# The last pair of forgetting-attention heads turned through VectorE and DRAM instead of on TensorE, with the filling jobs dealt anew

## The chip, the cores and the metric

The kernel runs on one core of one Trainium2 chip. The metric is device time in microseconds (us) for one launch; the median of three runs is compared. Engines are named as in the profile: PE is TensorE (PEld its weight loads), DVE is VectorE, ACT is ScalarE, POOL is GpSimd, SP is SyncE, which here only issues DMAs.

## The reference

One layer of a streaming encoder over 512 tokens of width 1024. Four token mixers run on the same normed input: differential attention (branch a), forgetting attention (branch f), a Conformer convolution (c) and a short gated convolution (d). Each is projected to 1024 channels, gated and summed; a cross-attention and a gated MLP follow. The part that the change touches is branch f, eight heads of width 64:

```python
c = jnp.cumsum(log_f, axis=1)                       # log_f: log-sigmoid of a gate column, per head
s = jnp.einsum('bqhd,bkhd->bhqk', q_blk, k) * scale
s = s + c_blk[..., None] - c_k[:, :, None, :]
p = jax.nn.softmax(jnp.where(mask, s, -jnp.inf), axis=-1)   # mask: key <= query
return jnp.einsum('bhqk,bkhd->bqhd', p, v)
...
proj = jnp.einsum('bsnc,ncd->bsnd', br, w_branch)   # br: the four branches, 512 channels each
gates = jax.nn.sigmoid(h @ w_gate + b_gate)
mixed = jnp.sum(gates * proj, axis=2) @ w_out
```

All is float32. The kernel gets this precision by splitting each factor into a high and a low part and multiplying three times (high by high, high by low, low by high).

## The kernel before

**Jobs.** `run_blocks` goes through a list of jobs. A typical job loads one 512 KB piece of weights (SP, tile `wr`, two buffers), splits it (ACT writes `wh` at L198, DVE writes `wl` at L199, four buffers each), and runs 24 matmuls of 128x128 by 128x512 (L241) into PSUM. Weights are fetched three jobs ahead.

**Background tasks.** Attention heads are generators, `f_task(p)` for a pair p of heads and `a_task(h)`, that are stepped between jobs by `Background`: it keeps a clock that advances with each matmul traced, pays a task's step from a credit, and takes up a step only when the delay that the last step gave has passed. At most two tasks are stepped at a time. `bg.drain` issues all the remaining steps of a task in one go. This settles the program order; a list scheduler then places each engine's instructions in a static order, by program order among what its own timeline holds ready. On the chip each engine, and SP's queue of DMAs, works strictly in that order.

**Forgetting attention.** `mixer_jobs` yields, for each pair p, two jobs that make the queries and keys (`kv_blocks(p)`; the second adds `f_task(p)`), and between the pairs jobs of branch a's gates and projection (`gate_blocks(0, "a")`, twelve jobs: twice a gate job and then a projection job, four times over). Before, three of them stand after pair 1, three after pair 2, six after pair 3, and then the drain of branch f. A step of `f_task` below 4 makes the scores of one strip of 128 queries against its (step+1)*128 keys for both heads: POOL makes the bias (L1123, L1125), PE the scores (`ps_sc`), DVE adds and finds the row extremum (L1129), ACT exponentiates (L1135), DVE and ACT normalise (L1137 to L1142). The strip, queries by keys, lies in a tile `e`, of which there are three buffers in all.

**Two ways of turning a strip.** The value product needs keys on the partitions. Pairs 0 to 2 (`far`) go a long way round: DVE transposes 32x32 squares (`turn_squares`, L854) into another `e`, `put` (L859) writes it to DRAM from SP, `get` (L866) reads it back in an order that finishes the turn, into `ptl`, and `split_in_place` makes the high part `pth` (ACT, L872) and the low part in place (DVE, L873). Pair 3 goes the short way: `to_keys_major` transposes each 128x128 block on PE into a bank `tr` (L247) and splits it out of PSUM (ACT L161, DVE L162). `GETS` and `SPLITS` say at which of the eight steps the strips are read back and split; the short way has six steps. `pth` and `ptl` have two buffers, one for each head of the pair, and hold two strips: strips 0 and 1, then 2 and 3.

**The end of a pair.** `values` multiplies the turned strips into two banks `av`, first strips 0 and 1, then 2 and 3. A last step adds each bank's halves (ACT copy L1153, DVE add L1154) and splits the pair's 128 channels into `y["f"]` (L161, L162).

**PSUM banks.** A job's bank comes from a rotation, `turn_of.among`. In this stretch it is `("mm", "mm", "tr0")`: two banks `mm` and one that the PE turns would use. Pair 3 sets it to `("mm")` at its step 2, as it needs both `tr` banks. After the drain come the jobs of the last branch, `last_branch_jobs`: two gate jobs of branch f, then `share("mm", "av")`, and then a projection job over `y["f"]` (two banks, each accumulated over four blocks of channels, one for each pair of heads), two gate jobs, and so on. A gate job's result goes to a tile `ge`, of two buffers, that its projection frees.

Of the kernel before, what the change touches and what calls it, by code (L numbers as in the profile page):

```python
# [83 lines left out]
def hybrid_layer(ctx: ExitStack, tc: tile.TileContext, a: dict, out: bass.AP):  # L84
# [21 lines left out]
    def share_now(*among):  # L106
        vars(turn_of).update(n=1, among=among)
# [102 lines left out]
    steps_of = []  # L210
# [654 lines left out]
    def get(d, n, pt, local):  # L865
        SP.dma_start(part_of(pt[1], n, local).bitcast(F32), d.rearrange("(a j) (b x) -> (j b) a x", j=32, b=4))  # L866

    def split_in_place(n, pt, local):
        hi, lo = (part_of(x, n, local) for x in pt)
        raw = lo.bitcast(F32)  # L870
        with tc.issue_after(evacuations[0]):
            A.copy(hi, raw)  # L872
        V.tensor_tensor(lo, raw, hi.bitcast(F32), ALU.subtract)  # L873
# [21 lines left out]
    def pt_tiles():  # L895
        return tuple(m1p.tile([P, 2, 4, 4, 32], F32R, tag=n, name=n, bufs=2) for n in ("pth", "ptl"))

    GETS, SPLITS = {3: (0, 1), 5: (2, 3)}, {4: (0, 1), 6: (2, 3)}
# [158 lines left out]
    f_steps = {-1: 8}  # L1057

    def f_task(p, qk, v):
        f_steps[p] = 0  # L1060
        far = p < 3
        while f_steps[p - 1] < 4:
            yield 0.0, 0.5
        ck = []
        for j in range(2):
            t = m1p.tile([P, S], F32, tag="ck", name="ck", bufs=2)
            G.dma_start(t, crows[2 * p + j:2 * p + j + 1, :].rearrange("a s -> (a s)").partition_broadcast(P))
            ck.append(t)
        yield 0.0, 2.0 if p else 5.0
        es, pts, av, ready = {}, None, None, []  # L1070

        def turn_ready():
            while ready:
                qt, e, w = ready.pop()
                turned = e4()
                for j in range(2):
                    turn_squares(turned[:, j, :w], e[:, j, :w])
                es[qt] = put(turned, w)
        for step in range(8 if far else 6):
            if step in ((5, 7) if far else (3, 5)):  # L1080
                if av is None:
                    av = [bank("av"), bank("av")]
                with tc.issue_after(steps_of[0]) if far else ExitStack():
                    for j in range(2):
                        hl = v[0][:, :, 2 * p + j]
                        values(av[j], lambda kt: ((hl[:, kt], 0), (hl[:, kt], 1)), pts[j],
                               step // 2 - (2 if far else 1))
            while step == (3 if far else 2) and f_steps[p - 1] < 8:
                yield 0.0, 0.5
            f_steps[p] = step + 1  # L1090
            cost = 0.0
            if step == 4:
                turn_ready()
            if far:
                for qt in SPLITS.get(step, ()):
                    for j in range(2):
                        split_in_place(qt + 1, pts[j], qt % 2)
                    cost += 0.1 + 0.3 * qt
                for qt in GETS.get(step, ()):
                    if qt % 2 == 0:  # L1100
                        pts = [pt_tiles() for _ in range(2)]
                    d = es.pop(qt)
                    for j in range(2):
                        get(d[:, j], qt + 1, pts[j], qt % 2)
            else:
                if step == 2:
                    share_now("mm")
                for qt in {2: (0, 1), 3: (2,), 4: (3,)}.get(step, ()):
                    if qt % 2 == 0:
                        pts = [pt_tiles() for _ in range(2)]  # L1110
                    e = es.pop(qt)
                    for j in range(2):
                        to_keys_major(e[:, j], qt + 1, pts[j], qt % 2)
                    cost += 0.4 + 0.3 * qt
            if step < 4:
                qt, w = step, (step + 1) * P
                e = es[qt] = e4()
                st = m1p.tile([P, 8], F32, tag="st8", name="st8", bufs=4)
                for j in range(2):
                    head = 2 * p + j  # L1120
                    bias = m1p.tile([P, S], F32, tag="fbias", name="fbias", bufs=2)

                    G.tensor_scalar(bias[:, :w], ck[j][:, :w], -1.0, cq[:, qt, head:head + 1],  # L1123
                                    ALU.mult, ALU.add)
                    G.affine_select(out=bias[:, w - P:w], in_=bias[:, w - P:w], pattern=[[-1, P]],  # L1125
                                    compare_op=ALU.is_ge, fill=BIG, base=0, channel_multiplier=1)
                    ps = bank("sc")
                    scores(ps, qk, j, qt * P, w)
                    low = V.tensor_tensor_reduce(e[:, j, :w], ps[:, :w], bias[:, :w], scale=-HD ** -0.5,  # L1129
                                                 scalar=3.0e38, op0=ALU.add, op1=ALU.min,  # L1130
                                                 accum_out=st[:, j:j + 1])
                with tc.issue_after(low.ins):
                    turn_ready()
                for j in range(2):
                    A.activation(e[:, j, :w], e[:, j, :w], AF.Exp, bias=st[:, j:j + 1],  # L1135
                                 scale=-1.0, accum_out=st[:, 4 + j:5 + j])
                V.reciprocal(st[:, 6:8], st[:, 4:6])  # L1137
                for j in range(2):
                    if j:
                        V.tensor_scalar(e[:, j, :w], e[:, j, :w], st[:, 6 + j:7 + j], None, ALU.mult)  # L1140
                    else:
                        A.activation(e[:, j, :w], e[:, j, :w], AF.Copy, scale=st[:, 6 + j:7 + j])  # L1142
                cost += 0.6 + 0.0038 * w
                if far:
                    ready.append((qt, e, w))
                    cost += 0.003 * w
            yield cost, 6.5 if far and step == 5 else 4.5
        if "f" not in y:
            y["f"] = (y8(), y8())

        e = e4()
        for j in range(2):
            A.copy(e[0:HD, j], av[j][HD:P])  # L1153
            V.tensor_tensor(e[j * HD:(j + 1) * HD, 0], av[j][0:HD], e[0:HD, j], ALU.add)  # L1154
        split(e[:, 0], y["f"][0][:, p], y["f"][1][:, p])
        yield 1.8, 0.0
# [45 lines left out]
    def mixer_jobs():  # L1202
        yield from c_jobs()
        yield then(lambda: bg.add(lam_task(), "lam"))
        yield from d_jobs()
        yield then(lambda: bg.add(conv_norm_task(), "conv"))
        wide = m1p.tile([P, NT, D], F32, tag="v", name="wide")
        free = iter([wide[:, i] for i in (0, 1, 2, 3) * 2])
        ns.out_sums = out_sums = Sums(w_out, NK // 2, lambda: next(free), SP, "out_sums")
        steps = {5: (out_sums.load, 0), 6: (out_sums.load, 1), 9: (out_sums.add, 0), 10: (out_sums.store, 0),  # L1210
                 11: (out_sums.add, 1)}
        for i, job in enumerate(gate_blocks(3, "d")):
            yield job
            if i in steps:
                yield then(lambda f=steps[i]: f[0](f[1]))
        yield then(lambda: y.pop("d"))
        vj = v_jobs(O_AV, va)
        yield then(lambda: (out_sums.store(1), out_sums.load(2), out_sums.load(3)) and None)
        for f, q in ((out_sums.add, 2), (out_sums.add, 3)):
            yield next(vj)  # L1220
            yield then(lambda f=f, q=q: f(q))
            yield then(lambda q=q: out_sums.store(q))
        yield from vj
        yield share("mm", "mm", "tr0")
        gc = gate_blocks(2, "c")
        for h, n in enumerate((0, 2, 4, 6)):
            yield from qk_jobs(O_AQ, O_AK, h, lambda qk, h=h: bg.add(a_task(h, qk, va), "a"))
            if n:
                yield then(lambda: bg.drain("conv"))
            for _ in range(n):  # L1230
                yield next(gc)
        yield then(lambda: bg.drain("a"))
        yield from vf_jobs(vf)
        yield from kv_blocks(0)
        ga = gate_blocks(0, "a")
        for p in range(1, 4):
            yield from kv_blocks(p)
            for _ in range((3, 3, 6)[p - 1]):
                yield next(ga)
        yield then(lambda: bg.drain("f"))  # L1240

# [656 lines left out]
```

## Time and profile before

| | |
|---|---|
| median of three runs | 1047.57 us (1047.52 to 1048.46) |
| the profiled execution's own time | 1047.26 us |
| its span, first to last instruction | 1045.5 us |
| PE busy | 1035.8 us, 5235 matmuls |
| DVE busy | 809.6 us |
| ACT busy | 510.6 us |
| POOL busy | 143.3 us |
| granted PE clock | 0.999 |
| pair 3's stretch, from its first scores to its last addition | 479.6 to 520.7 us |

Busy time counts each instruction from its start to its end, overlaps once; for PE, whose matmuls are pipelined, the distance between starts says more of what one costs than its duration. A time without a row's shape is a mean over shapes. "Idle before, releaser" in a row names what an engine waited for.

### The profile page before, as it was taken

How to read it: one execution, taken by the hardware profiler on the slowest of the kernel's cores; microseconds unless marked ns; L12 is line 12 of the kernel's file. 1: busy time of each engine (PE TensorE's matmuls, PEld its weight loads, DVE VectorE, ACT ScalarE, POOL GpSimd, SP SyncE). 2: the span in 40 equal slices, each digit the busy share in tenths (PEclk: the TensorE clock that was granted, in tenths of full speed). 3: DMA queues.
4: the chain of work that ended last, by engine and by line, in shares of the span. 5: the costliest groups of instructions: out<-in, count | busy, mean ns of one | idle time of the engine just before them, and what ended most of it. 6: DMA issues, size and time to landing. Idle time of an engine off the chain costs nothing.

```text
span 1045.5 us, 14417 instructions
## 1 busy us (share of the span) xinstructions
PE 1035.8 (99%) x5235; PEld 880.7 (84%) x5235; DVE 809.6 (77%) x1241; ACT 510.6 (49%) x838; POOL 143.3 (14%) x239
## 2 busy tenths in 40 slices
PE   9999999999999999999999999999999999999997
PEld 8888888888888988888888899998888888888886
DVE  7999998677787367878577898777767777667786
ACT  5322222376565365666444566555343333445662
POOL 4001000100010123342101031121112111111001
PEclk9999999999999999999999999999999999999999
DMA  8954333334433246666338744135676676626662
GB/s 271 311 156 100 101 101 101 91 91 121 142 104 109 62 122 178 184 165 158 120 124 287 237 134 127 62 108 184 193 240 229 214 227 217 220 82 183 216 214 82
DMA packets 187453, 166.48 MB, mean 159 GB/s; under 512 B 20415, under 2 KB 159148, under 8 KB 187381
## 3 DMA queue, kind: packets, MB, share of 16 engines
q1 hardware_dynamic: 178339, 133.80, 43.1%
q10 hardware_dynamic: 6482, 23.21, 6.1%
q0 software_dynamic: 2560, 8.54, 2.7%
q8 instruction: 41, 0.67, 0.3%
q14 instruction: 31, 0.25, 0.1%
HBM read 140.74 MB, written 24.79 MB: 158 GB/s over the span
## 4 chain that ended last, share of the span: by engine, by line
PE 99%; DMA 0%; DVE 0%; issue 0%; POOL 0%; POOLq 0%; DVEq 0%; SPq 0%; ACT 0%; ACTq 0%
PE ps_mm L241 47%; PE ps_av L241 30%; PE ps_tr L241 11%; PE ps_sc L241 7%; PE ps_tr L247 2%; PE ps_mm L459 1%; PE ps_av L459 1%; DMA xs<-in_x 0%; PE ps_tr L443 0%; DVE o L1788 0%; PE ps_av L443 0%; DVE nt L438 0%; DVE ge L1183 0%; DVE nt L412 0%; POOL st_m L285 0%
## 5 line engine op out<-in xcount | busy, mean ns | idle before, releaser
L198 ACT CAST wh<-wr 128x1024 fp32r<-128x1024 f32 (+1 forms) x140 | 146.5, 1047 | 233.5 <-PE ps_mm L241 121.2
L199 DVE TENSOR_TENSOR wl<-wr,wh 128x1024 fp32r<-128x1024 f32 (+1 forms) x140 | 174.8, 1249 | 86.2 <-ACT wh L198 85.4
L241 PE MATMUL ps_mm<-hth,wh 128*128 128x512 f32 (+1 forms) x536 | 198.9, 378 | 0.0
L241 PE MATMUL ps_mm<-htl,wh 128*128 128x512 f32 (+1 forms) x536 | 198.3, 377 | 0.0
L241 PE MATMUL ps_mm<-hth,wl 128*128 128x512 f32 (+1 forms) x536 | 198.3, 377 | 0.0
L241 PE MATMUL ps_av<-hth,wh 128*128 128x512 f32 (+1 forms) x328 | 122.5, 374 | 0.0
L241 PE MATMUL ps_av<-htl,wh 128*128 128x512 f32 (+1 forms) x328 | 122.5, 373 | 0.0
L241 PE MATMUL ps_av<-hth,wl 128*128 128x512 f32 (+1 forms) x328 | 122.3, 373 | 0.0
L241 PEld LDWEIGHTS ps_mm<-hth,wl 128*128 128x128 f32 x536 | 99.0, 188 | 18.3
L241 PEld LDWEIGHTS ps_mm<-hth,wh 128*128 128x128 f32 x536 | 99.0, 188 | 17.9 <-ACT hth L161 0.3
L241 PEld LDWEIGHTS ps_mm<-htl,wh 128*128 128x128 f32 x536 | 98.9, 188 | 17.9
L694 DVE SCALAR_TENSOR_TENSOR y<-y,par,y 128x508 f32<-128x508 f32 (+29 forms) x120 | 82.5, 725 | 0.1
L241 PEld LDWEIGHTS ps_av<-hth,wh 128*128 128x128 f32 x328 | 61.6, 188 | 11.1 <-DVE e L1154 0.3
L241 PEld LDWEIGHTS ps_av<-htl,wh 128*128 128x128 f32 x328 | 61.6, 188 | 10.9
L241 PEld LDWEIGHTS ps_av<-hth,wl 128*128 128x128 f32 x328 | 61.6, 188 | 10.9
L1689 DVE TENSOR_TENSOR wl<-dw,wh 128x1024 fp32r<-128x1024 f32 x32 | 40.2, 1260 | 15.0 <-ACT wh L1688 14.7
L1688 ACT CAST wh<-dw 128x1024 fp32r<-128x1024 f32 x32 | 33.4, 1051 | 22.2 <-PE ps_mm L241 7.4
L1636 ACT ACTIVATE th<-c 128x512 f32<-128x512 f32 x22 | 13.9, 632 | 48.8 <-DVE c L621 48.8
L1123 POOL TENSOR_SCALAR fbias<-ck,cq 128x128 f32<-128x128 f32 (+3 forms) x32 | 23.4, 739 | 73.0 <-DVE st L1129 66.6
L621 DVE SCALAR_TENSOR_TENSOR c<-ps_mm,par,c 128x510 f32<-128x510 f32 (+1 forms) x44 | 32.7, 744 | 0.7
L241 PE MATMUL ps_tr<-hth,wh 128*128 128x512 f32 x80 | 31.8, 398 | 0.0
L241 PE MATMUL ps_tr<-htl,wh 128*128 128x512 f32 x80 | 31.6, 395 | 0.0
(503 smaller groups left out, 2227.9 us busy)
## 6 DMA issues: line engine op xcount, KB each, us to landing
wr<-in_w_up SPq DMA_DIRECT2D x44, 512.0 KB
wr<-in_w_in SPq DMA_DIRECT2D x38, 512.0 KB
wr<-in_w_gate SPq DMA_DIRECT2D x32, 512.0 KB
wp<-in_w_down ACTq DMA_DIRECT2D x22, 512.0 KB
sums<-wp ACTq DMA_DIRECT2D x22, 512.0 KB
dw<-sums SPq DMA_DIRECT2D x44, 256.0 KB
wr<-in_w_branch SPq DMA_DIRECT2D x16, 512.0 KB
wide<-in_w_out SPq DMA_DIRECT2D x12, 512.0 KB
```

Of the source, the lines that this page charges most:

```text
L198: last_weights[:] = [order(A.copy(hi, raw[:, :n])).ins, low.tensor_tensor(lo, raw[:, :n], hi.bitcast(F32), ALU.subtract).ins]
L199: low.tensor_tensor(lo, raw[:, :n], hi.bitcast(F32), ALU.subtract).ins]
L241: steps_of[:] = [PE.matmul(ps, lhs, rhs, start=start, stop=stop).ins]
L247: turns.append(PE.transpose(ps, x, ident[:n, :n]).ins)
L459: keep(PE.matmul(banks[c][:, :S // 2], w[p == 1][:, k, c * P:(c + 1) * P], ht[p == 2][:, i * 4 + k, :S // 2], start=(i, p, k) == (0, 0, 0) ...
L621: ins = V.scalar_tensor_tensor(dst[:, s:], src[:, :S - s], w(k), dst[:, s:], ALU.mult, ALU.add)
L694: ins = V.scalar_tensor_tensor(dst[:, s:], src[:, :S - s], pc("conv_dw", k * 4 + j), dst[:, s:], ALU.mult, ALU.add)
L1123: G.tensor_scalar(bias[:, :w], ck[j][:, :w], -1.0, cq[:, qt, head:head + 1], ALU.mult, ALU.add)
L1636: A.activation(th, c[:, 0], AF.Silu)
L1688: A.copy(hi, x)
L1689: V.tensor_tensor(lo, x, hi.bitcast(F32), ALU.subtract)
```

## The change

Pair 3 takes the long way like the others: the short branch of `f_task` is gone, with its PE turns and its change of the bank rotation, and the task has eight steps with the delays of the others. The gate and projection jobs of branch a are dealt out two, three and seven in place of three, three and six, so that one job moves from behind pair 1 to behind pair 3 and the pairs 2 and 3 are begun one job earlier.

```diff
     def f_task(p, qk, v):
         f_steps[p] = 0
-        far = p < 3
...
-        for step in range(8 if far else 6):
-            if step in ((5, 7) if far else (3, 5)):
+        for step in range(8):
+            if step in (5, 7):
                 if av is None:
                     av = [bank("av"), bank("av")]
-                with tc.issue_after(steps_of[0]) if far else ExitStack():
+                with tc.issue_after(steps_of[0]):
                     for j in range(2):
                         hl = v[0][:, :, 2 * p + j]
                         values(av[j], lambda kt: ((hl[:, kt], 0), (hl[:, kt], 1)), pts[j],
-                               step // 2 - (2 if far else 1))
-            while step == (3 if far else 2) and f_steps[p - 1] < 8:
+                               step // 2 - 2)
+            while step == 3 and f_steps[p - 1] < 8:
                 yield 0.0, 0.5
...
-            if far:
-                for qt in SPLITS.get(step, ()):
...
-            else:
-                if step == 2:
-                    share_now("mm")
-                for qt in {2: (0, 1), 3: (2,), 4: (3,)}.get(step, ()):
-                    if qt % 2 == 0:
-                        pts = [pt_tiles() for _ in range(2)]
-                    e = es.pop(qt)
-                    for j in range(2):
-                        to_keys_major(e[:, j], qt + 1, pts[j], qt % 2)
-                    cost += 0.4 + 0.3 * qt
+            for qt in SPLITS.get(step, ()):
+                for j in range(2):
+                    split_in_place(qt + 1, pts[j], qt % 2)
+                cost += 0.1 + 0.3 * qt
+            for qt in GETS.get(step, ()):
+                if qt % 2 == 0:
+                    pts = [pt_tiles() for _ in range(2)]
+                d = es.pop(qt)
+                for j in range(2):
+                    get(d[:, j], qt + 1, pts[j], qt % 2)
...
-                cost += 0.6 + 0.0038 * w
-                if far:
-                    ready.append((qt, e, w))
-                    cost += 0.003 * w
-            yield cost, 6.5 if far and step == 5 else 4.5
+                ready.append((qt, e, w))
+                cost += 0.6 + 0.0068 * w
+            yield cost, 6.5 if step == 5 else 4.5
...
         for p in range(1, 4):
             yield from kv_blocks(p)
-            for _ in range((3, 3, 6)[p - 1]):
+            for _ in range((2, 3, 7)[p - 1]):
                 yield next(ga)
```

The tables and functions of the long way, which the change leaves as they are:

```python
GETS, SPLITS = {3: (0, 1), 5: (2, 3)}, {4: (0, 1), 6: (2, 3)}

def put(e, w):
    ...
    SP.dma_start(d, e[:, :, :w])
    return d
def get(d, n, pt, local):
    SP.dma_start(part_of(pt[1], n, local).bitcast(F32), d.rearrange("(a j) (b x) -> (j b) a x", j=32, b=4))
```

More of the change, by code (lines that the diff above doesn't have):

```diff
@@ L1093, in f_task @@
                 turn_ready()
-            if far:
-                for qt in SPLITS.get(step, ()):
-                    for j in range(2):
-                        split_in_place(qt + 1, pts[j], qt % 2)
-                    cost += 0.1 + 0.3 * qt
-                for qt in GETS.get(step, ()):
-                    if qt % 2 == 0:
-                        pts = [pt_tiles() for _ in range(2)]
-                    d = es.pop(qt)
-                    for j in range(2):
-                        get(d[:, j], qt + 1, pts[j], qt % 2)
-            else:
-                if step == 2:
-                    share_now("mm")
-                for qt in {2: (0, 1), 3: (2,), 4: (3,)}.get(step, ()):
-                    if qt % 2 == 0:
-                        pts = [pt_tiles() for _ in range(2)]
-                    e = es.pop(qt)
-                    for j in range(2):
-                        to_keys_major(e[:, j], qt + 1, pts[j], qt % 2)
-                    cost += 0.4 + 0.3 * qt
+            for qt in SPLITS.get(step, ()):
[8 more added lines that the diff above has]
+                    get(d[:, j], qt + 1, pts[j], qt % 2)
             if step < 4:
```

## The prediction

> **What bounds the kernel now.** I read the page first, then the stretches around pair 3, then PE's waits.
>
> ```profile
> span 1045.5 us, 14417 instructions
> PE 1035.8 (99%) x5235; PEld 880.7 (84%) x5235; DVE 809.6 (77%) x1241; ACT 510.6 (49%) x838; POOL 143.3 (14%) x239
> PE 99%; DMA 0%; DVE 0%; issue 0%; POOL 0%; POOLq 0%; DVEq 0%; SPq 0%; ACT 0%; ACTq 0%
> ```
>
> PE is busy for 99% of the span and the chain that ended last is 99% PE. Stretch by stretch (columns: sum of the stretch, then PE, PEld, DVE, ACT, POOL, clock, DMA share):
>
> ```profile
> 480.00:490.00 10.00, 10.00 (x48) 8.33 (x48) 8.52 (x19) 4.89 (x12) 4.72 (x8) 1.00 0.90 232
> 490.00:500.00 10.00, 10.00 (x55) 8.63 (x54) 8.09 (x19) 6.91 (x16) 4.53 (x6) 1.00 0.45 122
> 500.00:510.00 10.00, 10.00 (x55) 8.43 (x53) 6.68 (x13) 6.93 (x14) 0.00 (x0) 1.00 0.55 161
> 510.00:520.00 10.00, 10.00 (x57) 8.55 (x56) 3.51 (x5) 3.33 (x5) 0.00 (x0) 1.00 0.18 52
> ```
>
> PE is full in all four. DVE has 1.5 us of 10 to spare at first and 6.5 at the end; the DMA engines fall from 0.90 to 0.18. What PE waited for in the whole run near this place is two weight loads:
>
> ```profile
> PEld ps_mm L241 <- DVE ge L1183: 0.5, 1, 0.5
> PEld ps_av L241 <- DVE e L1154: 0.3, 1, 0.3
> ```
>
> So here an edit counts in two ways only: by the PE time that it takes away, and by any moment at which PE, which follows a fixed order, is made to wait.
>
> **The change part by part.** *The PE turns go.* The chain of waits over 488 to 530 us shows them as pieces of the time that decides:
>
> ```profile
> 491.67 0.22 PE ps_tr L247 x2
> 500.23 0.22 PE ps_tr L247 x2
> 501.16 0.22 PE ps_tr L247 x2
> 506.60 0.35 PE ps_tr L247 x3
> 508.52 0.35 PE ps_tr L247 x3
> 510.50 0.44 PE ps_tr L247 x4
> 514.63 0.44 PE ps_tr L247 x4
> ```
>
> 2 x (1+2+3+4) = 20 transposes in seven pieces, 3 x 0.22 + 2 x 0.35 + 2 x 0.44 = 2.24 us. All of it is on the path. If both waits above went as well (0.5 + 0.3), the saving would be 3.0 us; I count none of them and take 2.3. By the Trainium skill, page "TensorE: Matmul & The Clock Gate", section "Part 4: PE-mode transpose", one 128x128 transpose costs about 275 ns in a kernel; an estimate from that is 20 x 0.275 = 5.5 us. The pieces say 0.11 each, because transposes overlap one another here, so the sum goes by the pieces.
>
> *The squares come.* DVE turns each strip of each head, by these rows:
>
> ```profile
> L854 DVE STREAM_TRANSPOSE e<-e 128x512 f32<-128x512 f32 x3 | 3.2, 1082 | 0.0
> L854 DVE STREAM_TRANSPOSE e<-e 128x384 f32<-128x384 f32 x2 | 1.6, 852 | 0.4 <-DMA turned<-e 0.4
> L854 DVE STREAM_TRANSPOSE e<-e 128x256 f32<-128x256 f32 x2 | 1.2, 621 | 0.0
> L854 DVE STREAM_TRANSPOSE e<-e 128x128 f32<-128x128 f32 x2 | 0.7, 382 | 0.0
> ```
>
> 2 x (1.082 + 0.852 + 0.621 + 0.382) = 5.87 us more on DVE, between about 484 and 506 us. DVE's idle time from 490 to 520 is 1.9 + 3.3 + 6.5 = 11.7 us, so I cost them at nothing on PE as a load; as a delay they are in the tail below. If the cover were gone, the low parts of weights (L199) behind them would come late. The splits are exchanged one for one, out of SBUF in place of PSUM: nothing.
>
> *Four writes and eight reads come on SP's queue.* At the rows' 0.36 to 0.5 us of issue (below) some 5 us in a queue that issues one or two weight loads in 10 us: nothing while weights are ahead.
>
> *The dealing and the banks.* The twelve jobs of branch a are the same matmuls in another order, and PE is full on both sides of the move: nothing. What it does is start pair 3 sooner. I followed the planner's arithmetic (matmuls, costs, delays as written in the code): pair 3's strips 0 and 1 are taken up half a job earlier than before, strip 2 before the drain instead of in it. Strip 3, the first value product of pair 3 and the second one of pair 2 stay in the drain. One gate job in `tr0` instead of `mm` saves at most the 0.5 us wait above and costs nothing that the trace shows.
>
> *The tail decides.* After the drain PE fills its time with the last branch: two gate jobs, half a projection (nine matmuls into an `mm` bank), a third gate job into the other `mm` bank. Then it needs an `av` bank, and pair 3 holds both until its sums are read.
>
> ```profile
> 515.37 0.28 PE L241 MATMUL ps_av<-pth,v 128*128 128x256 f32 x1
> 518.58 0.69 PE L241 MATMUL ps_av<-y,wh 128*128 128x512 f32 x2
> 517.16 0.58 ACT L1153 COPY e<-ps_av 64x512 f32<-64x512 f32 x1 [1.47 <-PE ps_av L241]
> 517.77 0.68 DVE L1154 TENSOR_TENSOR e<-ps_av,e 64x512 f32<-64x512 f32 x1 [1.36 <-ACT e L1153]
> ```
>
> The first `av` bank is free at 517.77 + 0.68 = 518.45, and PE enters it at 518.58: the slack is 0.1 us. With 2.24 us less to do PE is there at 516.3. If the bank is free by then the saving stays; each us later costs one.
>
> When is it free on the long way? The rows I go by:
>
> ```profile
> 501.10 0.69 DVE L1129 CUSTOM_DVE_ANT_0 e<-ps_sc,fbias 128x512 f32<-128x512 f32 x1 [0.17 <-PE ps_mm L241]
> 494.83 2.85 POOL L1123 TENSOR_SCALAR fbias<-ck,cq 128x512 f32<-128x512 f32 x2 [4.87 <-DVE st L1129]
> 393.08 0.37 SPq L859 DMA_DIRECT2D turned<-e  x1
> 396.09 0.92 SPq L866 DMA_DIRECT2D ptl<-turned  x2
> 403.63 0.91 SPq L866 DMA_DIRECT2D ptl<-turned  x2
> 405.77 0.41 ACT L872 CAST pth<-ptl 128x256 fp32r<-128x256 f32 x1 [2.49 <-DMA ptl<-turned]
> 481.98 0.37 SPq L859 DMA_DIRECT2D turned<-e  x1
> 486.27 0.91 SPq L866 DMA_DIRECT2D ptl<-turned  x2
> 490.79 0.62 ACT L872 CAST pth<-ptl 128x512 fp32r<-128x512 f32 x1 [1.71 <-DMA ptl<-turned]
> 506.05 4.10 SPq L182 DMA_DIRECT2D wr<-in_w_gate  x2
> ```
>
> Before, strip 3's scores were added at 501.10 just after the PE turns of strip 1 (501.16 in the chain) gave back one of the three `e` buffers. Squares give it back sooner, so strip 3 is held only by its bias, ready near 494.83 + 2.85 + 0.6 = 498.3; with a share of DVE's queue its scores are done near 499.0. Then, by the three `e` buffers: squares of strip 2 (2 x 0.85) to 500.7; pair 2's closing additions and split (0.58 and 0.68 twice, then 0.62 and 0.69, overlapped: 3.4) to 504.1; squares of strip 3 (2 x 1.08) to 506.3; a write and a read, X; cast 0.62, low part 0.69, eight value matmuls 0.95, then 0.58 and 0.68 and a hand-over of 0.1. That is 506.3 + X + 3.6 = 509.9 + X, and PE waits when X is over 6.4 us.
>
> X has two ends. Light: a write of strip 0 from 393.08 to its read at 396.09, 3.0, and a read from 403.63 to its cast at 405.77, 2.1: X = 5.1, free at 515.0. Loaded: 481.98 to 486.27 and on to 490.79, 8.8: free at 518.7, a wait of 2.4 and a saving of about nothing. The loaded rows were taken at a DMA share of 0.90; pair 3's last strip will travel between 506 and 515, where before has 0.55 falling to 0.18. It is nearer to light, though its 512 KB are four times strip 0's; I take X near 6 and no wait.
>
> The sum: 2.3 us off the profiled execution's 1047.26 (span 1045.5 and 1.76 around it) is 1044.96; the median stands 0.31 above that execution, so 1047.57 - 2.3 = **1045.3 us**.
>
> **The rivals.** *Turned into a wait.* X between 6.4 and 10.7 us, or the same lateness in any link: the wait eats the saving to the point where it is 2.1 us worse, 1045.5 to 1049.7; at X = 8.8, 1047.7. For it: slack in this tail is 0.1 us now, and ACT already waits 1.71 and 2.49 us for such reads, so the fixed order thinks them quicker than they are. Against: DMA and DVE empty out after 500 us.
>
> *Slower: the read of the last strip is stuck in SP's queue.* SP issues in order, and the second of two loads at 506.05 goes out only some 3.7 us after the first, when a `wr` buffer is free. If strip 3's write or read stands behind such a load, X is 8.8 + 4.1 = 12.9, the bank is free at 522.8, PE stands for 6.5 us, less 2.3: 1051.8 us. It decides from X = 10.8 on. For it: three buffers of `e`, two of `wr`, one queue. Against: three heads of branch a and three pairs went this way, and PE's waits name no read and no split of theirs, though none of them had the end of branch f behind it. By the Trainium skill, page "VectorE: DVE Perf Modes", section "Rules for kernel authors", a 128x128 transpose belongs on TensorE where PSUM will do, which is the path given up here; the trace agrees on the engines' time (four blocks 1.08 us on DVE, 0.44 on PE), and says that DVE has that time to spare.
>
> *The transposes cost their full duration.* If PE's pieces understate them by the page's figure named above, the saving would be 5.5 us, 1042.1 us. The seven pieces speak against it.
>
> **How the numbers follow.** No wait (1044.5 to 1045.4): 0.50. Turned into a wait: 0.24. Slower: 0.23, a third of it below 1050.0. Full duration: 0.03. The range 1044.3 to 1050.0 leaves out the last and two thirds of the slower case, 0.03 + 0.15; the likeliest case's own range is 1044.3 to 1045.4. A measurement of this kernel can tell about 0.2%, 2.1 us, from no change. Faster by more: 0.50 + 0.03 = 0.53; within: 0.24; slower by more: 0.23.
>
> **What would show it.** These rows of before change:
>
> ```profile
> L247 PE MATMUL ps_tr<-ident,e x66: 201/272/301, 284.5 to 514.8; 128*128 128x128 f32 x62, 8*128 8x8 f32 x4
> L854 DVE STREAM_TRANSPOSE e<-e x36: 358/738/1115, 238.6 to 480.9; 128x128 f32<-128x128 f32 x9, 128x256 f32<-128x256 f32 x9, 128x384 f32<-128x384 f32 x9, 128x512 f32<-128x512 f32 x9
> L866 SPq DMA_DIRECT2D ptl<-turned x36: 359/440/1007, 240.7 to 486.7; - x36
> L859 SPq DMA_DIRECT2D turned<-e x24: 332/359/456, 239.1 to 482.0; - x24
> ```
>
> In the profile after: twenty fewer L247 of `ps_tr<-ident,e` (66 to 46), eight more L854 of `e<-e` (36 to 44), four more L859 and eight more L866; PE busy near 1033.5. Right: no PE wait over 0.5 us between 490 and 530, and pair 3's first L1153 by 515.2 us. Turned into a wait: PEld waiting for DVE L1154 or ACT L872 there. Slower: a PE gap of 4 us or more, with L866 of strip 3 issued after 511 behind a `wr` load. I am wrong altogether if PE's busy time does not fall, or if the time is lost before 490 us, where only the dealing acts.

## The result, and the profile after

The changed kernel takes 1054.97 us (median of four runs, 1054.06 to 1055.49) against 1047.55 for the kernel before: a ratio of 1.0070, 95% interval 1.0057 to 1.0083. It is 7.4 us slower. 1045.3 was forecast, and the range ended at 1050.0.

From the page of the changed kernel: span, busy times, the chain that ended last.

```profile
span 1053.2 us, 14415 instructions
PE 1037.5 (99%) x5215; PEld 880.9 (84%) x5215; DVE 813.9 (77%) x1249; ACT 510.8 (49%) x838; POOL 140.6 (13%) x239
PE 95%; DMA 2%; DVE 2%; issue 1%; SPq 0%; ACT 0%; POOL 0%; POOLq 0%; DVEq 0%; ACTq 0%
```

The span is 7.7 us longer. PE runs twenty matmuls fewer (5215 for 5235) and is yet busy 1.7 us longer. The chain that was PE for 99% is now 2% DMA and 2% DVE. The work itself changed as the code says; these rows, by line and shape (column after the count: shortest, mean and longest in ns), answer to the last four of the prediction:

```profile
L247 PE MATMUL ps_tr<-ident,e x46: 201/272/294, 284.6 to 382.1; 128*128 128x128 f32 x42, 8*128 8x8 f32 x4
L854 DVE STREAM_TRANSPOSE e<-e x44: 367/731/1120, 238.7 to 508.3; 128x128 f32<-128x128 f32 x11, 128x256 f32<-128x256 f32 x11, 128x384 f32<-128x384 f32 x11, 128x512 f32<-128x512 f32 x11
L866 SPq DMA_DIRECT2D ptl<-turned x44: 359/458/1637, 240.7 to 515.1; - x44
L859 SPq DMA_DIRECT2D turned<-e x28: 332/359/1179, 239.1 to 509.4; - x28
```

Up to 500 us PE is full in both traces. By stretches (sum of the stretch, then PE, PEld, DVE, ACT, POOL, clock, DMA share, GB/s):

```profile
500.00:510.00 10.00, 8.95 (x40) 6.62 (x38) 5.32 (x9) 6.57 (x15) 0.00 (x0) 1.00 0.55 173
510.00:520.00 10.00, 8.16 (x37) 6.30 (x37) 3.76 (x6) 1.86 (x4) 0.00 (x0) 1.00 0.99 249
520.00:530.00 10.00, 7.46 (x23) 5.83 (x24) 4.45 (x6) 3.67 (x6) 0.00 (x0) 0.66 0.17 52
```

From 500 us on PE is no longer full, the DMA share in 510 to 520 is 0.99 where before had 0.18, and in the last stretch the granted clock is 0.66. What PE's weight loads waited for between 490 and 535 us (total, times, longest):

```profile
PEld ps_av L241 <- ACT pth L872: 3.8, 4, 1.8
PEld ps_av L241 <- DVE ptl L873: 2.7, 4, 1.4
PEld ps_av L241 <- DVE e L1140: 1.2, 1, 1.2
PEld ps_mm L241 <- DVE y L162: 0.2, 1, 0.2
```

7.9 us in all, nearly all of it at pair 3's value products and at the projection behind them: high parts, low parts, the closing addition (L1140 is the old L1154; lines behind `f_task` moved up by 12 to 14). In the chain over 520 to 540 us stands the other loss:

```profile
523.31 0.60 DVE e L1140
523.96 8.47 PE ps_av L241 x24
535.84 2.72 PE ps_mm L241 x12
```

The twelve matmuls from 535.84 take 0.227 us each; 24 of them would take 5.44, and the 24 from 523.96 took 8.47: 3.0 us of halved clock. The sum: 2.2 saved, 7.9 - 0.8 = 7.1 of new waits, 3.0 of slow clock, together 7.9 longer by this count, and 7.7 by the spans. The split between waits and clock is rough: by the pages PE idles 6.0 us more (1053.2 - 1037.5 against 1045.5 - 1035.8) and is busy 1.7 us more, although its work shrank by 2.2.

Where the lateness comes from is read from the chain over 505 to 523 us, then from the timeline of that stretch for ACT, DVE, PE and POOL:

```profile
499.79 7.43 DMA turned<-e
...
509.36 3.06 DMA turned<-e
512.44 0.36 SPq L866
512.89 0.57 SPq L182
513.55 1.47 SPq L866
515.08 5.39 DMA ptl<-turned
```

```profile
504.22 0.30 ACT L872 CAST pth<-ptl 128x128 fp32r<-128x128 f32 x1 [3.38 <-DMA ptl<-turned]
504.54 1.07 ACT L1139 COPY e<-ps_av 64x512 f32<-64x512 f32 x2
504.55 0.29 DVE L873 TENSOR_TENSOR ptl<-ptl,pth 128x128 fp32r<-128x128 f32 x1 [3.51 <-ACT pth L872]
507.24 2.09 DVE L854 STREAM_TRANSPOSE e<-e 128x512 f32<-128x512 f32 x2 [0.23 <-DMA turned<-e]
517.10 0.62 ACT L872 CAST pth<-ptl 128x512 fp32r<-128x512 f32 x1 [0.32 <-DMA ptl<-turned]
520.49 0.62 ACT L872 CAST pth<-ptl 128x512 fp32r<-128x512 f32 x1 [0.17 <-DMA ptl<-turned]
521.16 0.39 PE L241 MATMUL ps_av<-pth,v 128*128 128x256 f32 x1 [1.63 <-ACT pth L872]
522.08 0.58 ACT L1139 COPY e<-ps_av 64x512 f32<-64x512 f32 x1
```

```profile
497.82 0.57 POOL L1252 DMA_DIRECT2D g_mem<-in_norm_mem  x1 [2.02 <-PE ps_sc L241]
498.57 0.54 POOL L1286 DMA_DIRECT2D m_t<-in_mem  x1 [0.17 <-issue]
```

Strip 2's write is issued at 499.79 and lands 7.43 us later, beside two 512 KB loads of the cross-attention's memory that POOL issued at 497.82 and 498.57. Its source is one of the three `e` buffers, so strip 3's squares could not start before it landed; they start at 507.24. The write is the last thing that they wait for, but by 0.23 us only. ACT meanwhile stands 3.38 us for a small read, with pair 2's closing copies behind it (504.54), and DVE stands 3.51 us for that cast (504.55), with pair 2's closing additions and the squares behind it.

From the end of the squares the chain runs on: 3.1 us for strip 3's write, 2.7 us (512.42 to 515.08) in which SP issues two other reads and a weight load, 5.4 us for the last read. At the end ACT casts head 0's last strip at 517.10, stands for head 1's reads, casts a weight, and only then copies the first `av` bank, at 522.08. PE's own order holds it up as well: head 1's value products stand ahead of the next projection, and the first of them waits 1.63 us for head 1's cast (521.16).

### The profile page after: what moved, and what is told of

The parts are those of the page before. It is cut to its first block, busy times and chain, and to the rows that moved or that the text cites. A ratio compares the mean times of both kernels' runs of the same rounds, so it can differ in the third digit from the quotient of the medians.

```text
span 1053.2 us, 14415 instructions
## 1 busy us (share of the span) xinstructions
PE 1037.5 (99%) x5215; PEld 880.9 (84%) x5215; DVE 813.9 (77%) x1249; ACT 510.8 (49%) x838; POOL 140.6 (13%) x239
## 4 chain that ended last, share of the span: by engine, by line
PE 95%; DMA 2%; DVE 2%; issue 1%; SPq 0%; ACT 0%; POOL 0%; POOLq 0%; DVEq 0%; ACTq 0%
PE ps_mm L241 44%; PE ps_av L241 30%; PE ps_tr L241 11%; PE ps_sc L241 7%; PE ps_tr L247 2%; DMA turned<-e 1%; PE ps_mm L459 1%; PE ps_av L459 1%; DMA ptl<-turned 1%; DMA xs<-in_x 0%; DVE e L854 0%; DVE wl L199 0%; ACT wh L198 0%; DVE ptl L873 0%; SPq L866 0%
## 5 line engine op out<-in xcount | busy, mean ns | idle before, releaser
L241 PE MATMUL ps_mm<-hth,wh 128*128 128x512 f32 (+1 forms) x528 | 195.3, 377 | 0.0
L241 PE MATMUL ps_mm<-htl,wh 128*128 128x512 f32 (+1 forms) x528 | 195.1, 377 | 0.0
L241 PE MATMUL ps_mm<-hth,wl 128*128 128x512 f32 (+1 forms) x528 | 195.0, 377 | 0.0
L241 PE MATMUL ps_tr<-hth,wh 128*128 128x512 f32 x88 | 34.8, 396 | 0.0
L241 PE MATMUL ps_tr<-htl,wh 128*128 128x512 f32 x88 | 34.7, 395 | 0.0
L241 PE MATMUL ps_tr<-hth,wl 128*128 128x512 f32 x88 | 34.7, 394 | 0.0
L873 DVE TENSOR_TENSOR ptl<-ptl,pth 128x128 fp32r<-128x128 f32 (+3 forms) x44 | 20.5, 499 | 16.9 <-ACT pth L872 16.7
```

The lines of the kernel that those rows point to most:

```text
L241: steps_of[:] = [PE.matmul(ps, lhs, rhs, start=start, stop=stop).ins]
```

## The experiments

Each was compared with the kernel before on its own chip: ratio (95% interval), median in us.

| run | edit | median | ratio |
|---|---|---|---|
| deal_only | before, dealt 2, 3, 7 | 1047.49 | 0.9998 (0.9988 to 1.0007) |
| far_336 | after, dealt 3, 3, 6 | 1056.38 | 1.0077 (1.0062 to 1.0092) |
| mem_late | after, memory loads later in program order | 1056.01 | 1.0071 (1.0054 to 1.0088) |
| pace_30 | after, shorter delays in all steps | 1052.45 | 1.0043 (1.0028 to 1.0058) |
| lead_55 | after, one delay 1 us shorter | 1049.57 | 1.0016 (1.0007 to 1.0026) |
| mem_late2 | after, memory loads on SP behind a later weight load | 1051.20 | 1.0034 (1.0021 to 1.0047) |
| own_tile | after, strip 3's squares in tiles of their own | 1054.46 | 1.0062 (1.0047 to 1.0077) |
| warm | after, ten filler matmuls in the waits | 1053.54 | 1.0052 (1.0036 to 1.0069) |
| comb | lead_55 and mem_late2 | 1045.39 | 0.9978 (0.9969 to 0.9987) |
| two_comb | comb, two gate jobs before the drain | 1046.67 | 0.9994 (0.9985 to 1.0003) |
| last_pe | after, strip 3 turned on PE | 1046.91 | 0.9995 (0.9986 to 1.0003) |
| last_pe_lead | last_pe and lead_55 | 1053.39 | 1.0054 (1.0041 to 1.0067) |
| before_comb | before, with comb's two edits | 1052.72 | 1.0039 (1.0027 to 1.0051) |
| comb_336 | comb, dealt 3, 3, 6 | 1052.24 | 1.0043 (1.0030 to 1.0056) |
| comb_45 | comb, the delay 2 us shorter | 1045.26 | 0.9979 (0.9970 to 0.9987) |

**deal_only** and **far_336** separate the two halves of the change.

```diff
-            for _ in range((3, 3, 6)[p - 1]):     # deal_only: in before; far_336: the other way round, in after
+            for _ in range((2, 3, 7)[p - 1]):
```

> The kernel before with only the jobs dealt two, three, seven; pair 3 still goes the short way. If the loss comes from the long way of pair 3 in the tail (lead theory): within 1.5 us of before, 1046 to 1049. If moving jobs is what costs: 1051 or more, with PE waits before 490 us or in the tail.

> The long way for pair 3 with the old dealing of three, three, six. Lead theory: pair 3 starts some 3 us later than in the changed kernel, so the PE waits and the slow clock between 500 and 530 us stay or grow: 1054 to 1059. If the dealing is what costs: 1045 to 1048.

The dealing alone is no change; the long way without it loses as much as with it. The loss belongs to the turning of pair 3.

**mem_late** and **mem_late2** take the memory loads out of the tail.

```diff
-        G.dma_start(ns.gain, a["norm_mem"][0].partition_broadcast(P))    # in open_last_branch
-        bg.add(mem_task(), "mem")
+    def start_mem():                               # called five jobs later
+        with tc.issue_after(last_load[0]):         # mem_late2 only: on SP, behind the newest weight load
+            SP.dma_start(ns.gain, a["norm_mem"][0].partition_broadcast(P))
+        bg.add(mem_task(), "mem")                  # mem_late2: mem_task's loads of m_t go to SP likewise
```

> The changed kernel with the loads of the memory tokens and their gain (two of 512 KB issued near 498 us) and their task begun five jobs later. If crowding by other transfers is what makes pair 3's writes and reads slow: the write of strip 2 lands within 4.5 us instead of 7.4 and the PE waits shrink by half or more, 1047 to 1051. Lead theory without crowding: under 1.5 us gained, 1053 to 1055.

> The changed kernel with the memory tokens' loads put into SP's queue behind a weight load that goes out after pair 3's reads; in the earlier try they stayed at 498 us. Crowding theory: the write of strip 2 lands in 4.5 us instead of 7.4 and the first reads sooner, PE waits shrink by 2 to 4 us: 1048 to 1052. Lead theory without crowding: 1053 to 1056.

mem_late tells nothing: the scheduler still issued the loads near 498 and 499 us. In mem_late2 they go out at 520.2 and 520.7, behind pair 3's reads, and its timeline shows what they had cost:

```profile
503.75 2.07 DVE L854 STREAM_TRANSPOSE e<-e 128x512 f32<-128x512 f32 x2
513.48 0.62 ACT L872 CAST pth<-ptl 128x512 fp32r<-128x512 f32 x1 [0.30 <-DMA ptl<-turned]
516.90 0.62 ACT L872 CAST pth<-ptl 128x512 fp32r<-128x512 f32 x1 [0.16 <-DMA ptl<-turned]
```

Strip 3's squares start 3.5 us sooner, although strip 2's write, the first of the two in SP's row below, is issued at the same moment: it was done within 4.0 us instead of 7.4 (the DMA engines stand at 0.01 from 502.0 to 503.7 us, where after has 0.93). ACT's wait of 3.38 us shrinks to 0.25. The edit moves the loads in time and to another queue at once, so which of the two helped isn't told apart.

```profile
499.80 6.41 SPq L859 DMA_DIRECT2D turned<-e  x2
```

That is 3.8 us of the time, and PE still waits 4.0.

**pace_30** and **lead_55** shorten the delays that the planner waits before it takes up a task's next step.

```diff
-            yield cost, 6.5 if step == 5 else 4.5
+            yield cost, 5.0 if step == 5 else 3.0     # pace_30
+            yield cost, 5.5 if step == 5 else 4.5     # lead_55
```

> The changed kernel with the steps of the forgetting-attention task given 3.0 us (5.0 after step 5) in place of 4.5 (6.5), so that by the planner's arithmetic pair 3's first value product and its last reads are issued before the drain. Lead theory: PE waits in the tail under 1.5 us, no slow clock, 2 us off before: 1045 to 1047. If the round trip hurts whatever its lead: 1052 or more.

> The changed kernel with 5.5 in place of 6.5 us after step 5, nothing else: by the planner's arithmetic a tick after a projection job is no longer missed, so pair 2's second product and pair 3's steps 2 and 3 come before the drain, some 8 us sooner. The faster pace of 3.0 took 2.5 us off and ended the slow clock, but made PE wait on a full DVE between 440 and 490 us. Lead theory: tail waits under 3 us, no slow clock, 1045 to 1049. Rival, the round trip outruns its place in PE's order whatever the lead: 1051 or more.

pace_30 gains 2.5 us and loses elsewhere part of what it wins at the end: between 440 and 490 us PE is now busy 47.85 us of 50 (50.0 in after), with waits for DVE's `st`, ACT's `pth` and DVE's `ptl`, whose work stands closer together there. lead_55 changes one pause (in every pair), keeps PE at 50.0 there, and gains more than mem_late2, 5.4 us:

```profile
502.24 2.08 DVE L854 STREAM_TRANSPOSE e<-e 128x512 f32<-128x512 f32 x2
511.32 0.62 ACT L872 CAST pth<-ptl 128x512 fp32r<-128x512 f32 x1 [0.43 <-DMA ptl<-turned]
514.81 0.62 ACT L872 CAST pth<-ptl 128x512 fp32r<-128x512 f32 x1 [0.21 <-DMA ptl<-turned]
```

**own_tile** gives strip 3's squares a place that waits for no write.

```diff
+                if p == 3 and qt == 3:          # in turn_ready: each head in a tile of the bias, written by itself
+                    own = m1p.tile([P, S], F32, tag="fbias", name="own", bufs=2)
+                    turn_squares(own[:, :w], e[:, j, :w]); SP.dma_start(d[:, j], own[:, :w])
```

> The changed kernel with strip 3's squares of pair 3 written to two bias tiles of their own, so that they need not wait until strip 2's write has left its buffer. Buffer theory: squares start near 506 instead of 507.2 and with no wait on a write, at most 1 to 2 us gained: 1052 to 1055. If the three buffers were the whole cause: 1046 to 1049.

The squares start at 505.95 and name no write any more, but pair 2's closing copies still stand behind the reads in ACT's order. Some 0.5 us came of it, which is inside the interval: the third buffer is one link among several of equal lateness.

**warm** keeps PE at work in the waits (the ten products go into a score bank and are used by nobody).

```diff
+                        if p == 3 and step == 7:
+                            ps = bank("sc")
+                            for _ in range((6, 4)[j]):
+                                d = PE.matmul(ps, ht[0][:, 0, :P], ht[0][:, 0], start=True, stop=True).ins
...
```

> The changed kernel with ten matmuls of no use (six before the second head's last product, four behind it) where PE waits 1.6 and 1.0 us; their result is not read. Clock theory (the waits halve the granted clock from 523 to 529.6 us, which costs 14 matmuls some 2.9 us): the clock stays at 1.00 and 2 to 3 us are gained, 1052 to 1053. If the slow clock is not due to the waits: 1055 or more.

The stretch of the halved clock, in warm:

```profile
520.00:530.00 10.00, 9.41 (x46) 7.25 (x45) 4.45 (x6) 4.92 (x8) 0.77 (x2) 1.00 0.21 64
```

46 matmuls (ten of them the fillers) instead of 23, at a clock of 1.00, and 1.4 us won against after. The halved clock was a cost of its own; the waits stay.

**comb** has the edits of lead_55 and mem_late2 together.

> The changed kernel with both edits that helped alone: the pause after step 5 is 5.5 instead of 6.5 us, and the memory loads stand in SP's queue behind the later weight load. Theory (the tail is a chain of DMA trips of pair 3, lengthened by crowding; the shorter pause issues its links sooner, the later memory loads make the trips shorter): the two act on different links, so most of 5.4 and 3.9 us come off together; with a floor where PE no longer waits: 1046.5 to 1048. Rival (both only give back the same halved clock, which a run of filler products showed to be worth 1.4 us, and the first few us of waits): the second edit adds little to the first, 1049 to 1050.

The stretch from 500 us, and the same three rows of its timeline:

```profile
500.00:510.00 10.00, 10.00 (x52) 8.48 (x51) 5.77 (x8) 4.98 (x8) 0.00 (x0) 1.00 0.96 249
510.00:520.00 10.00, 10.00 (x50) 8.37 (x49) 3.53 (x6) 4.00 (x6) 0.00 (x0) 1.00 0.45 157
520.00:530.00 10.00, 10.00 (x46) 8.29 (x45) 7.32 (x11) 3.82 (x6) 0.77 (x2) 1.00 0.21 63
```

```profile
497.70 2.07 DVE L854 STREAM_TRANSPOSE e<-e 128x512 f32<-128x512 f32 x2
506.43 0.62 ACT L872 CAST pth<-ptl 128x512 fp32r<-128x512 f32 x1 [0.34 <-DMA ptl<-turned]
509.95 0.62 ACT L872 CAST pth<-ptl 128x512 fp32r<-128x512 f32 x1 [0.24 <-DMA ptl<-turned]
```

PE waits for nothing between 490 and 535 us. The kernel is 2.0 us faster than before, which it beats with an interval clear of 1. Beside the rows of the other kernels it shows what moved. From the end of the squares to the two casts it takes 7.8 and 11.2 us in after (509.33 to 517.10 and 520.49), 7.7 and 11.1 in mem_late2, 7.0 and 10.5 in lead_55, 6.7 and 10.2 in comb. The trip hardly changes; the start of it does: the squares end at 509.3, 505.8, 504.3 and 499.8, and the medians follow in that order.

**two_comb** puts more of PE's other work beside the trips: two gate jobs go ahead of the drain.

```diff
+        ns.gf = gate_blocks(1, "f", mix_place, mix_done)
+        yield next(ns.gf); yield next(ns.gf)        # and not again in last_branch_jobs
         yield then(lambda: bg.drain("f"))
```

> As comb, and the first two gate jobs of the last branch stand ahead of the point where PE's other work waits for branch f, so PE has two more jobs (16 products of 0.227 us each, 3.6 us apiece) to lie beside pair 3's trips. Theory (PE runs out of work 3 to 8 us before the last values are there): what is left of the waits goes, 1045.5 to 1046.5, which is before less the twenty transposes. Rival (the scheduler's order, not the amount of other work, leaves the gap: ACT and DVE hold the drain behind reads in their own order): no better than comb.

It is no better than comb, as the rival said; but comb has no wait left to fill, so the run can't decide between the two. (A gate job is 24 products, 5.4 us, and not the 16 of the expectation.) Two waits are there that comb hasn't: 1.1 us for the closing addition (L1140), as both closing additions now stand together at 516.87 where comb has the first at 511.22, and 1.0 us for a gate tile (L1169) at 568.8, far behind the tail.

**last_pe** and **last_pe_lead** leave only the last strip on PE.

```diff
                 for j in range(2):
-                    get(d[:, j], qt + 1, pts[j], qt % 2)
+                    if p == 3 and qt == 3:
+                        to_keys_major(d[:, j], 4, pts[j], 1)
+                    else:
+                        get(d[:, j], qt + 1, pts[j], qt % 2)
...                                             # and no squares for it; share_now("mm") at pair 3's step 3
```

> The changed kernel, but strip 3 of pair 3 is turned on PE as before (8 of the 20 transposes), strips 0 to 2 by squares and DRAM. Theory (the end of branch f waits for strip 3's write and read, and these come last because strip 2's write holds the third e buffer): the last trip is gone, only strip 2's is left and it has one step more of time; the waits of the tail fall under 1 us, and 12 transposes of 0.112 us are saved: 1046 to 1048. Rival (crowding: 20 of the 36 strips' pieces and the memory loads still meet at 494 to 510, so strip 2's read comes late and ACT's order holds all behind it): 1050 to 1054.

> As last_pe with the pause after step 5 at 5.5 us. Theory: with the last trip gone the pause is no longer on the chain, so this is within 1 us of last_pe. Rival (strip 2's read is now the last link and the pause stands behind it or before it): another 2 to 4 us off.

Without the last trip 8 of the 9.6 us between after and comb are won back; PE's largest wait there is now 1.7 us, for strip 3's own scaling before its turn. last_pe_lead was a miss of both theories: the same pause that gained 5.4 us in lead_55 costs 6.5 here. PE waits 2.5 us for a `pth` near 500 us, at a clock of 0.83 in 500 to 510, and then, near 579 us and far behind the tail, 1.8 and 1.1 us for split weights, at a clock of 0.66 in 580 to 585. Why the earlier step puts the weights' splits late in this order and not in comb's was not followed up.

**before_comb**, **comb_336** and **comb_45** ask whether comb's gain is the change's.

```diff
-            yield cost, 6.5 if far and step == 5 else 4.5     # before_comb: in before, and the loads as in mem_late2
+            yield cost, 5.5 if far and step == 5 else 4.5
-            yield cost, 5.5 if step == 5 else 4.5             # comb_45: in comb
+            yield cost, 4.5
```

> The kernel before (pair 3 on PE, jobs dealt out three, three, six) with the two edits of comb. Theory (the gain of comb is the transposes that PE no longer makes): PE has under 1 us of waits here to win back, so 1046.8 to 1048.5, and comb stays 2 us below it. Rival (the two edits gain by themselves, whatever pair 3 does): 1044.5 to 1046, level with comb.

> comb with the jobs dealt out three, three, six as in the kernel before. Theory (dealing changes only where a job stands and not the tail, as in the two runs on it): within 1 us of comb, 1044.5 to 1046.5. Rival (two, three, seven gives pair 3 the half job that the tail needs): PE waits of 1 to 3 us come back, 1046.5 to 1049.

> comb with the pause after step 5 at 4.5 us, the same as after the other steps. Theory (the pause is a link of the chain only while the chain is late; with no wait left a shorter one brings nothing, but puts the splits before their reads in ACT's and DVE's order, for all four pairs): PE waits for ACT pth or DVE ptl of 1 to 4 us come back, 1046 to 1050. Rival (shorter is better still, since the splits come off the tail): 1044 to 1045.5.

In the kernel before the two edits cost 5.0 us, so they are no gain by themselves. The loss is not in the tail, where PE waits as in before (0.5 and 0.3 us). PE's longest wait in the run, which ends at 574.79:

```profile
PEld ps_av L241 <- DVE ge L1183: 2.8, 1, 2.8
```

The longest piece of the chain over 560 to 580 us is a read of the memory task (`mn<-turned_m`, from 563.39), of 7.35 us. ACT and DVE wait for it (DVE for 6.8 us), a gate tile stands behind them in DVE's order, PE waits for the gate tile, and its clock is 0.83 in 570 to 580. The memory loads had gone out at 521.13 and 521.62, where before had them near 498, so the later loads are the likely reason; but mem_late2 sends them as late and has no such wait, and the two edits weren't tried apart. So this run doesn't say what they are worth to before's tail. comb_336 contradicts what deal_only seemed to settle: beside the two edits the dealing is worth 6.9 us, 1052.24 against comb's 1045.39. Its PE waits are back:

```profile
PEld ps_av L241 <- DVE e L1140: 1.6, 1, 1.6
PEld ps_av L241 <- ACT pth L872: 1.5, 2, 1.1
PEld ps_av L241 <- DVE ptl L873: 1.1, 2, 0.5
```

Its squares of strip 3 start at 505.74 where comb's start at 497.70. comb_45 is as fast as comb (1045.26), so a still shorter pause brings nothing and costs nothing.

## Why the prediction was wrong, by its own steps

**The PE turns: right.** The counts are as forecast (46, 44, 28, 44 rows). comb, with no wait left in the stretch, runs PE 1034.2 us busy against 1035.8, and its median, 1045.39, is 2.0 us below before, with an interval of 1.4 to 3.2 us around the 2.3 that the prediction took. In the profiled executions, 2.8 us apart in span, 1.6 of it is PE's busy time and 1.2 less idling, so how well the totals agree is partly luck. "PE busy near 1033.5" failed in after (1037.5) in the main because matmuls at half clock count longer, 3.0 of the 4.0 us.

**The squares as a load and the splits' exchange: right. The issues: not nothing.** No wait of PE names a weight's low part. But on the chain stand 2.7 us of SP's issuing between the landing of strip 3's write and the last read: a read of 0.36, a weight load of 0.57 and a read of 1.47 us, where the prediction counted 0.36 to 0.5 each and all of it hidden.

**The dealing at nothing: right alone, wrong in company.** By itself it moves neither kernel; once the tail is tight it decides 6.9 us (comb against comb_336).

**The tail: this is the step that failed.** It forecast the first `av` bank free at 509.9 + X with X = 6, 515.9, against a need at 516.3. The copy came at 522.08 and the addition ended at 523.9, 8.0 us later. Two terms make that up:

- *The start.* The squares of strip 3 were to end at 506.3, with strip 2's write not on the chain at all and pair 2's closing additions from 500.7 on. They ended at 509.3, 3.0 us late. Beside the memory loads strip 0's read kept ACT waiting 3.38 us, with the closing copies and additions behind it, and strip 2's write took 7.4 us and held the third buffer; by either way the squares were free at nearly the same time (0.23 us apart), which fits that own_tile, which frees the squares from the write alone, won almost nothing. mem_late2, without the loads, starts the squares at 503.75, where 504.1 was forecast: the arithmetic of the buffers was sound, the transfers in it were unpriced. The prediction looked for crowding on SP's queue and did not ask what POOL would start in that stretch, though the memory loads were in the trace of before.
- *The trip.* X was priced as one write and one read, near the light end, 3.0 + 2.1 us. A pair has two heads. Head 0's cast came after 7.8 us, head 1's after 11.2, and the copy that frees head 0's bank stands behind head 1's casts in ACT's order, as the next projection stands behind head 1's value products in PE's. So the X that counts was 11.2, 5.2 more than taken, and above the "loaded" end of 8.8. Of it the write was 3.1, as at the light end; the issues were 2.7 and the last read 5.4. X is 10.2 even in comb, where the memory loads go out behind the last read, so it isn't crowding by those. But the premise that the DMA engines would be half empty failed as well: their share in 510 to 520 us was 0.99, not 0.18. Two weight loads of 512 KB, issued at 510.47 and 512.89, went beside strip 3's write (512 KB) and the four reads (896 KB), so they were some 1.0 of the 2.5 MB that 249 GB/s make in that stretch. comb has two such loads beside its trip too (500.90 and 503.37, share 0.96). No run took them away, so how much of X is the reads' own length and how much the weights' traffic stays open.

8.2 us from the two terms, 8.0 measured. X = 11.2 lies past the 10.8 that the slower rival named as its point of decision. That rival's mechanism was not the one, since the `wr` load ahead of head 1's reads held SP for 0.6 us, not for the 4.1 of a missing buffer, and no single wait was over 1.8 us; its price of 6.5 us of waiting was near the 7.1 found. "Turned into a wait" named the right rows (PEld waiting for L872 and the closing addition) and too small a size.

**The halved clock: not in the sum.** 3.0 us by the chain; warm, which removes it, gained 1.4 us net of its ten fillers. The clock in 520 to 530 us is 0.66 in after and far_336, 0.73 in mem_late, 0.83 in mem_late2 and own_tile, 0.75 in comb_336; in lead_55, whose 4.1 us of waits lie spread over 490 to 520, it is 1.00. It should have been a second term of each rival: waits close together cost their length and then a stretch of half speed.

**What the runs settle.** The saving is there and was lost to a chain that starts too late. The order is fixed before the run, and in it the last trip starts too late for its length; starting it 9.6 us earlier takes all of the loss away. What stays open is what the reads would take without weight loads beside them, and why so small a change of a delay shifts the static order by so much, and in either direction (lead_55 against last_pe_lead).

## What to carry to other kernels

When work moves from an engine to a trip through memory at the end of a task, write the chain for every head and buffer that shares it, and look on all queues for what else the schedule starts in that window. A stage whose order is fixed ahead of time must start the trip early enough for its measured length; here the trip stayed nearly as long (11.2 to 10.2 us), and the time followed its start. And an edit found neutral by itself is not neutral in company: test the parts of a schedule change also together with the repair.

## What the runs showed of the hardware that had not been expected

The clock was halved without any long pause of PE. In after, by single microseconds (PE's busy time stands second, the granted clock third from the end):

```profile
519.00:520.00 1.00, 0.53 (x6) 0.39 (x4) 0.00 (x0) 0.19 (x1) 0.00 (x0) 1.00 0.35 82
520.00:521.00 1.00, 0.00 (x0) 0.00 (x0) 0.56 (x1) 0.83 (x2) 0.00 (x0) 1.00 0.00 0
521.00:522.00 1.00, 0.50 (x2) 0.30 (x3) 0.69 (x1) 1.00 (x2) 0.00 (x0) 1.00 0.00 0
522.00:523.00 1.00, 0.93 (x7) 0.78 (x7) 0.91 (x1) 0.68 (x3) 0.00 (x0) 1.00 0.00 0
523.00:524.00 1.00, 0.04 (x1) 0.04 (x1) 0.97 (x3) 0.55 (x1) 0.00 (x0) 0.52 0.00 0
529.00:530.00 1.00, 1.00 (x5) 0.77 (x4) 0.00 (x0) 0.00 (x0) 0.00 (x0) 0.57 0.00 0
```

From 519 to 524 us PE was idle for 3.0 us of 5, in pieces of which the longest was 1.6 us, and from about 523 to 529.6 the clock was 0.50, with PE full from 524 on. By the Trainium skill, page "TensorE: Matmul & The Clock Gate", section "HAM oscillation — how this bites in real kernels", the rule is to leave no idle gap of PE over about 3.4 us; here no gap was half as long, so by this trace short waits close together are enough. In before_comb a single pause of 2.4 us, which ended at 574.79, was followed by a clock of 0.50 from 576 to 578 us.

A write of 384 KB to DRAM took 7.4 us beside two 512 KB loads issued from POOL and at most 4.0 us without them (after and mem_late2, issued at the same moment).
